# Weights' rounded high parts by a second transfer from GpSimd's queue, low parts on VectorE

## The chip, the cores and the metric

The kernel runs on 1 core of one Trainium2 chip. The metric is the device time of one execution in microseconds (us). Three runs of the kernel before took 629.13 us at the median, 628.03 to 631.23. One further execution was profiled; everything said of stretches and waits comes from it. What differs by less than 0.5% counts as no change.

## The reference

Two layers of a streaming encoder over 512 tokens of width 1024, in float32. Layer A is multi-head latent attention with a low-rank query and a low-rank key/value, a rotary key shared by 8 heads and a gate. Layer B is differential attention: two softmaxes per head, their weighted difference, a norm per head, a gate. Between them one shared K/V is projected from the residual stream.

```python
u = rmsnorm(h, pre_g); proj = u @ w_in                       # layer A
c_q, c_kv, k_r, z = split(proj, [768, 1280, 1344])
q = rmsnorm(c_q, q_norm_g) @ w_uq                            # 8 heads of 128 + 64 rotary
k_n = rmsnorm(c_kv) @ w_uk; v = rmsnorm(c_kv) @ w_uv
p = softmax(mask((q_n k_n + q_r k_r) * scale)); o = p @ v    # chunk-causal, chunk 64
h = h + rmsnorm((o * silu(z)) @ w_o, post_g)
k, v = split(rmsnorm(h) @ w_kv); k = rope(k)                 # shared K/V
q, z = split(rmsnorm(h) @ w_in); q = rope(q)                 # layer B
p = softmax(q1 k1) - lam * softmax(q2 k2); o = p @ v
o = rmsnorm(o, subln_g) * (1 - lam_init)
h = h + rmsnorm((o * silu(z)) @ w_o, post_g)
```

## The kernel before

Every product of weights is made of three passes on TensorE (PE): each operand is cut into a high part, rounded to PE's type `float32r`, and a low part, operand less high part, and `mm3` (L181 to L185) adds high x high, high x low and low x high into one PSUM tile. A weight block is 128 rows by up to 1024 columns (512 KB); a projection of one head with 1024 input channels takes 24 products of 128x128 by 128x512.

The class `Stream` holds all weight blocks in the order of their use. `load` (L80) brings a raw block by SyncE's (SP's) DMA queue into one of 2 buffers `wr`. `split` (L92) makes the high part in `wh` and the low part in `wl`, 3 buffers each, or in places of their own (`w1h`, `w1l` for the second half of the output projections, `sp` for some others). `ahead`, called behind each use, loads three and splits two blocks ahead of the block in use. So the high part of block k+3 can be written when PE's last product with the high part of block k is done.

Which engine splits is set by `eng`. For the first projection (g0, the compressed key/value) and the two blocks split with it, both parts come from VectorE (DVE). Behind L359 the high part is a `tensor_scalar` with 1.0 on GpSimd (POOL, L129) and the low part a subtraction on DVE (L132). In layer B the blocks of k and of the gate z have both parts on POOL, the blocks of q have the rule's.

POOL also multiplies the rotations' second halves by the sines (L374), scales exponentials by 1 / sum (L545 in layer A, L877 in layer B), sums squares (L343, L394, L407), applies the norm of some heads (L906) and stores the residual rows into `hdr` by its own DMA queue (L716). DVE does the rotations' other parts (L372, L373, L375), the scores' scaling with the maximum (L516), the weighted difference of the two softmaxes (L878) and all low parts of activations (L132, L832, L835). ScalarE (ACT) rounds activations and takes exponentials.

The tile framework's scheduler puts each engine's instructions in an order of its own, by a simulated timeline; on the chip each engine runs its instructions in that order, and an instruction that waits holds those behind it. Tiles in PSUM come from 8 buffers; a product into a new one waits until the old content was read.

Layer B's heads run as listed in `border`: the projections k0, q0, k1, z0, then the scores s0, then q1, k2, z1, z2, z3, and from then on for each head h the scores s(h+1), the projection q(h+2), the transposes t(h), k(h+3), perhaps a gate block, and the products with V, p(h).

Of the kernel before, what the change touches and what calls it, by code (L numbers as in the profile page):

```python
# [33 lines left out]
# columns of the small table  # L34
# [7 lines left out]
# 2*pi in parts of few bits, so that n * part is exact  # L42
# [16 lines left out]
def f(ap):  # L59
    return ap.bitcast(F32)  # L60


class Stream:
    """Weight blocks in the order of their use: loaded ahead, split one ahead."""

    def __init__(self, nc, raw, wh, wl):
        self.nc, self.rawp, self.pools = nc, raw, (wh, wl)
        self.units, self.raw, self.done = [], {}, {}
        self.n_load = self.n_split = self.n_get = 0
        self.eng = ("dve", "dve")  # L70
        self.first = {}     # the places of the first units
        self.tailed = set()

# [18 lines left out]
    def split(self, upto):  # L92
        self.load(upto)
        while self.n_split < min(upto, len(self.units)):
            k = self.n_split
            to = [self.units[k][1](n, k) for n in range(2)]
            if to[0] is None:       # its place isn't there yet
                return
            raw = self.raw.pop(k)
            kc, m = raw.shape[1], raw.shape[2]  # L100
            if k in self.tailed:    # the last 64 columns' low part goes behind their high part
                hi, lo = (t[:, None, :m + 64] for t in to)
                self.nc.vector.tensor_copy(hi[:, :, :m], raw)
                for a, o in ((0, lo[:, :, :m - 64]), (m - 64, hi[:, :, m:])):
                    v = slice(a, a + o.shape[2])
                    self.nc.vector.tensor_tensor(o, raw[:, :, v], f(hi[:, :, v]), op=ALU.subtract)
            else:
                hi, lo = (t[:, :kc * m].rearrange("p (k m) -> p k m", k=kc) for t in to)
                split(self.nc, hi, lo, raw, *(self.units[k][2] or self.eng))
            self.done[k] = (hi, lo)  # L110
            self.n_split += 1
# [12 lines left out]
def split(nc, hi, lo, src, eng="act", lo_eng="dve"):  # L124
    """hi = src to the product's type, lo = src - hi: exact together."""
# [16 lines left out]
def _body(ctx, tc, nc, ins, out, dbg):  # L142
# [38 lines left out]
    def mm3(o, w, x, first, last):  # L181
        """o += w^T x, each of w and x a (high, low) pair."""
# [4 lines left out]
    # ------------------------------------------------------------ first loads  # L187
# [4 lines left out]
    # the first chunk in two parts, for the products to start early  # L192
# [73 lines left out]
    # ------------------------------------------------------------ constants  # L266
# [12 lines left out]
    # products that nobody reads, to have TensorE's clock up when the first data come  # L279
# [9 lines left out]
    def rsqrt_rows(r, v2):  # L289
        """r = (2 v2)^-1/2 by the tables, then one step of Newton"""  # L290
# [15 lines left out]
    # ------------------------------------------------------------ x and the first projection  # L306
# [52 lines left out]
    ws.eng = ("pool", "dve")  # L359
# [8 lines left out]
    # ------------------------------------------------------------ c_q, and c_kv's norm beside it  # L368
    def rope(src, C, Sn, shuf):
        """the rotated src (PSUM) in a new tile"""  # L370
# [27 lines left out]
    # the rotary key: its weights' high part on one half of the rows, the low part on the other  # L398
# [40 lines left out]
    # ------------------------------------------------------------ the gate  # L439
# [25 lines left out]
    # ------------------------------------------------------------ V  # L465
    vh, vl = big_t("vh"), big_t("vl")      # [token, (tile, half), 512]
# [13 lines left out]
    # ------------------------------------------------------------ attention, layer A  # L480
# [24 lines left out]
    def softmax_part(h, tags, srcs, nscale):  # L505
        """masked scores (one PSUM tile per query tile) to exponentials and 1 / their sums"""
        e = [epool.tile([P, 1280], F32, tag="e", name=f"e{tag}{h}") for tag in tags]
        st = [[sm_t(n + tag) for n in ("mx", "l", "ri")] for tag in tags]
        for i in range(NT):
            n = P * (i + 1)  # L510
            one = slice(i, i + 1)
            for et, (mx, l, _), src in zip(e, st, srcs):
                ev = et[:, OFF[i]:OFF[i] + n]
                o = src(i)
                # the negated logits, their least, and exp(least - negated logit)
# [32 lines left out]
    PT = [(0, 0), (512, 1), (1024, 2), (896, 3)]     # where key tile j starts in the transposed tile  # L548
# [71 lines left out]
    def post(parts, done=None):  # L620
        """res += norm(o) * g, one token tile, by parts of its row: (o, g, res, a tile for o * g)"""
# [22 lines left out]
    def wo_end(norm, done, cut=False):  # L644
        """the last heads' products with w_o, one token tile after the other"""
# [9 lines left out]
        for i in range(NT):  # L655
            wo_half0(w, 7, [i])
            if cut and i == NT - 1:
                # in two parts, for the sums of squares to end early
# [16 lines left out]
    def attention(order, zg, proj, scores, norm, after):  # L675
        """the heads, one behind the other, and the first products with w_o beside the last ones"""
# [27 lines left out]
    # ------------------------------------------------------------ output projection A, h, its transpose  # L704
# [77 lines left out]
    # lambda  # L782
# [29 lines left out]
    # ------------------------------------------------------------ layer B: attention  # L812
# [42 lines left out]
    def scores_b(h):  # L855
# [3 lines left out]
        def src(i):  # L859
            """both scores' products: query high and low parts below each other, by the key's  # L860
            high part on either half of the rows, then the query's high part by the key's low part"""
# [22 lines left out]
    def subln_sq(h, o):  # L884
        sq = tmp_t("sqo")
        if h < H - 1:
            # the squares of either half of the rows, added, high and low part below each other
# [49 lines left out]
def _mt(w):  # L937
    """(K, 128 m) to [m, 128, K / 128, 128]"""
# [4 lines left out]
def _half(w):  # L943
    """(K, 1024) to [half, pair, 128, 2, 512]"""
# [66 lines left out]
```

## Time and profile before

| What | us |
|---|---|
| median of three runs (lowest, highest) | 629.13 (628.03, 631.23) |
| the profiled execution: span, the only time that its page gives | 628.3 |
| PE busy | 599.2 |
| DVE busy | 445.2 |
| ACT busy | 254.2 |
| POOL busy | 246.1 |
| share of the chain that ended last: PE, DVE, ACT, POOL, DMA | 69%, 15%, 5%, 3%, 2% |

The span runs from the first to the last instruction. Busy time counts the time in which an engine has an instruction running; DMA-issuing instructions are not counted. PEclk is the TensorE clock that was granted, as a share of full speed. The profile's idle times carry the name of what ended them. A row of a tile gives shortest, median and longest duration.

### The profile page before, as it was taken

What the parts mean: (1) busy time and instruction counts of PE and PEld (TensorE: products, weight loads), DVE (VectorE), ACT (ScalarE), POOL (GpSimd) and SP (SyncE); (2) the same over time, 40 slices, a digit from 0 to 9 for tenths busy, and PEclk for the clock granted to TensorE, in tenths of its full rate; (3) what the DMA queues carried; (4) which work ended last, traced back from release to release, by engine and by line L of the source; (5) the groups of instructions that cost most, each with busy time, mean ns of one, the idle gap of its engine ahead of it and who ended that gap; (6) DMA issues with size and microseconds to landing.
All of it is one profiled execution on the core that took longest, in us unless ns stands there. A gap on an engine that the chain in (4) does not pass through costs nothing.

```text
span 628.3 us, 7754 instructions
## 1 busy us (share of the span) xinstructions
PE 599.2 (95%) x2742; PEld 485.9 (77%) x2742; DVE 445.2 (71%) x790; ACT 254.2 (40%) x560; POOL 246.1 (39%) x232
## 2 busy tenths in 40 slices
PE   8998999999999999999999996999989999899995
PEld 6776888888888888788878884877768677587785
DVE  7997963346574758756775277748997897988754
ACT  6045411222343434313661124164645539637341
POOL 5251541113343231443232555737346554545100
PEclk9997999999999999999999997999889799699999
DMA  8132242312221223555312231140221121126102
GB/s 305 35 130 68 67 135 101 93 58 71 82 67 43 68 92 96 200 147 162 101 43 80 89 101 67 38 131 33 68 67 35 34 76 59 34 94 215 61 34 101
DMA packets 20119, 56.24 MB, mean 90 GB/s; under 512 B 2416, under 2 KB 3056, under 8 KB 20080
## 3 DMA queue, kind: packets, MB, share of 16 engines
q1 hardware_dynamic: 19296, 53.51, 26.9%
q0 software_dynamic: 640, 2.10, 0.9%
q8 instruction: 22, 0.36, 0.2%
q14 instruction: 17, 0.14, 0.1%
q10 hardware_dynamic: 144, 0.13, 0.1%
HBM read 51.53 MB, written 4.19 MB: 89 GB/s over the span
## 4 chain that ended last, share of the span: by engine, by line
PE 69%; DVE 15%; ACT 5%; issue 5%; POOL 3%; DMA 2%; SPq 1%; DVEq 0%; POOLq 0%; ACTq 0%
PE wo L183 4%; PE wo L185 4%; PE wo L184 4%; PE qb L183 3%; PE qb L184 3%; PE qb L185 2%; PE za L183 2%; PE za L184 2%; PE za L185 2%; DVE eb L878 2%; PE vb L183 2%; PE vb L184 2%; PE vb L185 2%; DVE ra L375 2%; PE cq L183 2%
## 5 line engine op out<-in xcount | busy, mean ns | idle before, releaser
L129 POOL TENSOR_SCALAR wh<-wr 128x1024 fp32r<-128x1024 f32 (+2 forms) x74 | 80.1, 1083 | 197.9 <-PE qb L184 31.3
L132 DVE TENSOR_TENSOR wl<-wr,wh 128x1024 fp32r<-128x1024 f32 (+2 forms) x60 | 72.6, 1211 | 34.6 <-POOL wh L129 34.5
L132 POOL TENSOR_TENSOR wl<-wr,wh 128x1024 fp32r<-128x1024 f32 x16 | 40.2, 2513 | 0.7
L375 DVE TENSOR_TENSOR ra<-ra,rb 128x512 f32<-128x512 f32 x21 | 32.1, 1527 | 5.4 <-POOL rb L374 5.4
L866 PE MATMUL sb<-k,q 128*128 128x128 f32 (+3 forms) x64 | 23.7, 419 | 11.7 <-DVE mxb L516 5.4
L545 POOL TENSOR_SCALAR ea<-ea,ria 128x128 f32<-128x128 f32 (+3 forms) x32 | 18.5, 595 | 36.5 <-DVE ria L522 36.5
L127 ACT ACTIVATE pth<-pt 128x512 fp32r<-128x512 f32 (+1 forms) x48 | 21.9, 529 | 25.0 <-PE pt L557 25.0
L878 DVE SCALAR_TENSOR_TENSOR eb<-eb,rib,ec 128x128 f32<-128x128 f32 (+3 forms) x32 | 30.7, 989 | 1.6 <-POOL ec L877 1.5
L877 POOL TENSOR_SCALAR ec<-ec,ric 128x128 f32<-128x128 f32 (+3 forms) x32 | 23.3, 744 | 18.4 <-DVE ric L874 15.5
L183 PE MATMUL qb<-hT2h,wh 128*128 128x512 f32 x64 | 30.1, 470 | 0.0
L184 PE MATMUL qb<-hT2l,wh 128*128 128x512 f32 x64 | 28.7, 448 | 0.0
L519 ACT ACTIVATE ea<-ea,mxa 128x128 f32<-128x128 f32 (+3 forms) x32 | 17.9, 560 | 25.9 <-DVE mxa L516 25.5
L185 PE MATMUL qb<-hT2h,wl 128*128 128x512 f32 x64 | 28.3, 441 | 0.0
L132 DVE TENSOR_TENSOR ptl<-pt,pth 128x512 fp32r<-128x512 f32 (+1 forms) x48 | 26.5, 590 | 1.8 <-ACT pth L127 1.8
L183 PE MATMUL wo<-w1h,ogh 128*128 128x512 f32 (+1 forms) x72 | 26.7, 371 | 0.0
L374 POOL TENSOR_TENSOR rb<-rb,SB 128x512 f32<-128x512 f32 x16 | 21.7, 1354 | 12.5 <-DVE rb L372 12.4
L185 PE MATMUL wo<-w1h,ogl 128*128 128x512 f32 (+1 forms) x72 | 26.5, 368 | 0.0
L183 PE MATMUL wo<-wh,ogh 128*128 128x512 f32 x64 | 25.4, 399 | 1.1 <-ACT ogh L127 1.1
L184 PE MATMUL wo<-w1l,ogh 128*128 128x512 f32 (+1 forms) x72 | 26.4, 366 | 0.0
L866 PEld LDWEIGHTS sb<-k,q 128*128 128x128 f32 x64 | 11.6, 202 | 18.8 <-DVE mxb L516 6.8
L183 PE MATMUL kb<-hT1h,wh 128*128 128x512 f32 x64 | 25.3, 396 | 0.0
L183 PE MATMUL za<-xh,wh 128*128 128x512 f32 x64 | 25.0, 391 | 0.0
(329 smaller groups left out, 1847.3 us busy)
## 6 DMA issues: line engine op xcount, KB each, us to landing
wr<-in_w_za SPq DMA_DIRECT2D x8, 512.0 KB, 3.6
wr<-in_w_oa SPq DMA_DIRECT2D x8, 512.0 KB, 3.6
wr<-in_w_vb SPq DMA_DIRECT2D x8, 512.0 KB, 3.6
wr<-in_w_kb SPq DMA_DIRECT2D x8, 512.0 KB, 3.5
wr<-in_w_qb SPq DMA_DIRECT2D x8, 512.0 KB, 3.5
wr<-in_w_zb SPq DMA_DIRECT2D x8, 512.0 KB, 3.5
wr<-in_w_ob SPq DMA_DIRECT2D x8, 512.0 KB, 3.7
wr<-in_w_cq SPq DMA_DIRECT2D x6, 512.0 KB, 3.5
```

What stands on the lines that cost most here:

```text
L127: nc.scalar.activation(hi, src, AF.Copy)
L129: nc.gpsimd.tensor_scalar(hi, src, 1.0, 1.0, op0=ALU.mult, op1=ALU.mult)
L132: (nc.vector if lo_eng == "dve" else nc.gpsimd).tensor_tensor(lo, src, f(hi), op=ALU.subtract)
L183: pe.matmul(o, w[0], x[0], start=first, stop=False)
L184: pe.matmul(o, w[0], x[1], start=False, stop=False)
L185: pe.matmul(o, w[1], x[0], start=False, stop=last)
L374: gps.tensor_tensor(b, b, Sn, op=ALU.mult)
L375: dve.tensor_tensor(a, a, b, op=ALU.add)
L545: gps.tensor_scalar(ev, ev, ri[:, i:i + 1], 1.0, op0=ALU.mult, op1=ALU.mult)
L866: pe.matmul(os[g][:, :n], qb[g][:, ti], kb[g][:, :n], start=True, stop=False)
L877: gps.tensor_scalar(e2[:, w], e2[:, w], r2[:, i:i + 1], 1.0, op0=ALU.mult, op1=ALU.mult)
L878: dve.scalar_tensor_tensor(e1[:, w], e1[:, w], r1[:, i:i + 1], e2[:, w], op0=ALU.mult, op1=ALU.subtract)
```

## The change

The stream gets a flag `cast`, set behind the first projection (where before the engines were set). With the flag, `split` begins a DMA on POOL's queue from the same place in DRAM into the high part's tile, whose type `float32r` has the transfer round, and the low part is a subtraction on DVE, whatever engines the block was added with. The raw block still comes by SP's queue; the low part needs both transfers. POOL makes no parts of weights any more. Comments of the file go too, and the lines behind L104 move down by up to 6 (L132 is L138, the rotation's L372 to L375 are L378 to L381, L516 is L522); the new transfer is L112 and the new subtraction L113.

```diff
@@ -61,15 +61,16 @@
         self.tailed = set()
+        self.cast = False
...
@@ -106,7 +107,12 @@
             else:
                 hi, lo = (t[:, :kc * m].rearrange("p (k m) -> p k m", k=kc) for t in to)
-                split(self.nc, hi, lo, raw, *(self.units[k][2] or self.eng))
+                if self.cast:
+
+                    self.nc.gpsimd.dma_start(hi, self.units[k][0])
+                    self.nc.vector.tensor_tensor(lo, raw, f(hi), op=ALU.subtract)
+                else:
+                    split(self.nc, hi, lo, raw, *(self.units[k][2] or self.eng))
             self.done[k] = (hi, lo)
...
@@ -356,7 +362,7 @@
-    ws.eng = ("pool", "dve")
+    ws.cast = True
```

The scheduler's order changes with it. PE's and SP's orders stay nearly as they were. Three places:

First extract: DVE behind the first projection, where the angles of layer B's rotation (`ang`, `SB`, `CB`) are made. `wl11` is the low part of the third block of c_q, `axl` and `akl` are low parts of sums of squares that PE adds up next. Before:

```order
L402 TENSOR_TENSOR kr_400<-g0_4_146,kr_400 128x512
L132 TENSOR_TENSOR wl11_453<-wr11_334,wh11_452 128x1024
L321 SCALAR_TENSOR_TENSOR ang_377<-n_379,ang_377 128x512
L322 TENSOR_SCALAR ang_377<-ang_377 128x512
L326 TENSOR_SCALAR SB_376<-SB_376,cols_90 128x512
L328 TENSOR_SCALAR CB_375<-CB_375,cols_90 128x512
L132 TENSOR_TENSOR wl12_489<-wr12_450,wh12_488 128x1024
L132 TENSOR_TENSOR axl_415<-acc_x_141,axh_414 128x512
```

and now:

```order
L408 TENSOR_TENSOR kr_400<-g0_4_146,kr_400 128x512
L327 SCALAR_TENSOR_TENSOR ang_377<-n_379,ang_377 128x512
L328 TENSOR_SCALAR ang_377<-ang_377 128x512
L113 TENSOR_TENSOR wl11_453<-wr11_334,wh11_452 128x1024
L332 TENSOR_SCALAR SB_376<-SB_376,cols_90 128x512
L334 TENSOR_SCALAR CB_375<-CB_375,cols_90 128x512
L138 TENSOR_TENSOR axl_415<-acc_x_141,axh_414 128x512
L138 TENSOR_TENSOR akl_419<-acc_kv_397,akh_418 128x512
```

The low part stands behind the last two steps of the angles, no longer ahead of them.

Second extract: POOL at the start of layer B, from the high part of k1's block (`wh65`) on; `wh66` is z0's, `wh67` q1's, `wh68` k2's, `wh69` z1's; each `rb` is the product with the sines in a rotation, `ec` the second softmax of head 0. Before:

```order
L129 TENSOR_SCALAR wh65_3121<-wr65_3064 128x1024
L132 TENSOR_TENSOR wl65_3122<-wr65_3064,wh65_3121 128x1024
L129 TENSOR_SCALAR wh66_3164<-wr66_3119 128x1024
L374 TENSOR_TENSOR rb_3105<-rb_3105,SB_376 128x512
L132 TENSOR_TENSOR wl66_3165<-wr66_3119,wh66_3164 128x1024
L129 TENSOR_SCALAR wh67_3210<-wr67_3162 128x1024
L374 TENSOR_TENSOR rb_3151<-rb_3151,SB_376 128x512
L129 TENSOR_SCALAR wh68_3242<-wr68_3208 128x1024
L374 TENSOR_TENSOR rb_3194<-rb_3194,SB_376 128x512
L132 TENSOR_TENSOR wl68_3243<-wr68_3208,wh68_3242 128x1024
L129 TENSOR_SCALAR wh69_3344<-wr69_3240 128x1024
L132 TENSOR_TENSOR wl69_3345<-wr69_3240,wh69_3344 128x1024
```

and now:

```order
L112 DMA wh65_3121<-in_w_kb 128x1024
L112 DMA wh66_3164<-in_w_zb 128x1024
L380 TENSOR_TENSOR rb_3105<-rb_3105,SB_376 128x512
L112 DMA wh67_3210<-in_w_qb 128x1024
L380 TENSOR_TENSOR rb_3151<-rb_3151,SB_376 128x512
L112 DMA wh68_3242<-in_w_kb 128x1024
L380 TENSOR_TENSOR rb_3194<-rb_3194,SB_376 128x512
L112 DMA wh69_3344<-in_w_zb 128x1024
L883 TENSOR_SCALAR ec0_3247<-ec0_3247,ric_3253 128x128
```

The order of high parts and rotations is the same; subtractions are gone from between them, and each high part is a transfer that POOL begins.

Third extract: DVE at the same place, from q0's rotation (`qb0`) over k1's (`kb1`) to the first scores of head 0 (`sb0_0_0`). Before:

```order
L373 TENSOR_TENSOR ra_3150<-qb0_3125,CB_375 128x512
L132 TENSOR_TENSOR wl67_3211<-wr67_3162,wh67_3210 128x1024
L375 TENSOR_TENSOR ra_3150<-ra_3150,rb_3151 128x512
L832 TENSOR_TENSOR q0_3156<-ra_3150,q0_3156 64x512
L832 TENSOR_TENSOR q1_3157<-ra_3150,q1_3157 64x512
L372 STREAM_SHUFFLE rb_3194<-kb1_3168 128x512
L373 TENSOR_TENSOR ra_3193<-kb1_3168,CB_375 128x512
L375 TENSOR_TENSOR ra_3193<-ra_3193,rb_3194 128x512
L835 TENSOR_TENSOR kl_3201<-ra_3193,k0_3199 64x512
L835 TENSOR_TENSOR kl_3201<-ra_3193,k1_3200 64x512
L516 ISA eb0_3246,mxb_3248<-sb0_0_0_3254,mask_126 128x128
L516 ISA mxb_3248 128x1
```

and now:

```order
L379 TENSOR_TENSOR ra_3150<-qb0_3125,CB_375 128x512
L381 TENSOR_TENSOR ra_3150<-ra_3150,rb_3151 128x512
L113 TENSOR_TENSOR wl67_3211<-wr67_3162,wh67_3210 128x1024
L838 TENSOR_TENSOR q0_3156<-ra_3150,q0_3156 64x512
L838 TENSOR_TENSOR q1_3157<-ra_3150,q1_3157 64x512
L378 STREAM_SHUFFLE rb_3194<-kb1_3168 128x512
L379 TENSOR_TENSOR ra_3193<-kb1_3168,CB_375 128x512
L381 TENSOR_TENSOR ra_3193<-ra_3193,rb_3194 128x512
L113 TENSOR_TENSOR wl68_3243<-wr68_3208,wh68_3242 128x1024
L841 TENSOR_TENSOR kl_3201<-ra_3193,k0_3199 64x512
L841 TENSOR_TENSOR kl_3201<-ra_3193,k1_3200 64x512
L522 ISA eb0_3246,mxb_3248<-sb0_0_0_3254,mask_126 128x128
```

q1's low part (`wl67`) has moved behind q0's rotation, and k2's (`wl68`), which POOL made, stands behind k1's. A third one, z0's (`wl66`), stands a few rows ahead behind k0's rotation, where there was none.

## Rows read from the trace of the kernel before

**Rows 1.** The page, part 1: busy us, share of the span, instructions of each engine.

```profile
PE 599.2 (95%) x2742; PEld 485.9 (77%) x2742; DVE 445.2 (71%) x790; ACT 254.2 (40%) x560; POOL 246.1 (39%) x232
```

**Rows 2.** PE's waits over the span: us in total, times, longest us.

```profile
PE sb L866 <- DVE mxb L516: 5.4, 2, 4.8
PE ssx L415 <- ACT axh L127: 4.0, 1, 4.0
```

**Rows 3.** Busy time by stretch, PE alone: stretch, length, busy (instructions), granted clock, DMA share, GB/s.

```profile
45.00:60.00 15.00, 11.03 (x35) 0.77 0.27 89
380.00:395.00 15.00, 10.18 (x33) 0.77 0.21 70
435.00:450.00 15.00, 14.26 (x51) 0.77 0.12 36
460.00:480.00 20.00, 17.93 (x76) 0.83 0.18 54
485.00:500.00 15.00, 13.55 (x45) 0.77 0.12 36
...
535.00:550.00 15.00, 13.11 (x35) 0.66 0.11 36
```

**Rows 4.** DVE's instructions in order of time: start, us, line, operation, tiles.

```profile
41.07 1.71 DVE L132 TENSOR_TENSOR wl<-wr,wh 128x1024 fp32r<-128x1024 f32 x1
...
364.39 2.87 DVE L375 TENSOR_TENSOR ra<-ra,rb 128x512 f32<-128x512 f32 x1 [0.91 <-POOL rb L374]
...
371.37 1.82 DVE L132 TENSOR_TENSOR wl<-wr,wh 128x1024 fp32r<-128x1024 f32 x1
373.12 1.53 DVE L375 TENSOR_TENSOR ra<-ra,rb 128x512 f32<-128x512 f32 x1
...
378.81 2.84 DVE L375 TENSOR_TENSOR ra<-ra,rb 128x512 f32<-128x512 f32 x1 [0.68 <-POOL rb L374]
...
383.65 2.19 DVE L835 TENSOR_TENSOR kl<-ra,k 64x512 fp32r<-64x512 f32 x1 [0.56 <-ACT k L830]
```

**Rows 5.** POOL's instructions in order of time: z0's cast, two of the 16 subtractions.

```profile
361.99 1.06 POOL L129 TENSOR_SCALAR wh<-wr 128x1024 fp32r<-128x1024 f32 x1 [1.69 <-PE kb L184]
...
378.74 2.37 POOL L132 TENSOR_TENSOR wl<-wr,wh 128x1024 fp32r<-128x1024 f32 x1
...
457.18 2.70 POOL L132 TENSOR_TENSOR wl<-wr,wh 128x1024 fp32r<-128x1024 f32 x1
```

**Rows 6.** DVE by shape, 350 to 600 us (busy us, mean ns), then two tiles' rows (shortest/median/longest ns).

```profile
L375 DVE TENSOR_TENSOR ra<-ra,rb 128x512 f32<-128x512 f32 x16 | 27.4, 1714 | 3.0 <-POOL rb L374 2.9
...
L835 DVE TENSOR_TENSOR kl<-ra,k 64x512 fp32r<-64x512 f32 x16 | 14.6, 916 | 5.2 <-ACT k L830 5.1
...
L375 DVE TENSOR_TENSOR ra<-ra,rb x21: 674/1446/2884, 72.6 to 556.7; 128x512 f32<-128x512 f32 x21
...
L132 DVE TENSOR_TENSOR wl<-wr,wh x60: 681/1220/2312, 32.3 to 585.8; 128x1024 fp32r<-128x1024 f32 x40, 128x768 fp32r<-128x768 f32 x12, 128x512 fp32r<-128x512 f32 x8
```

**Rows 7.** POOL by shape, 350 to 600 us: count, busy us, mean ns, idle before.

```profile
L132 POOL TENSOR_TENSOR wl<-wr,wh 128x1024 fp32r<-128x1024 f32 x15 | 37.8, 2521 | 0.6
L129 POOL TENSOR_SCALAR wh<-wr 128x1024 fp32r<-128x1024 f32 x27 | 32.1, 1188 | 49.8 <-PE qb L184 31.3 <-PE kb L184 6.9 <-PE vb L185 6.3
```

**Rows 8.** DMA issues: POOL's issuing instruction (ns), then count, KB each, us to landing.

```profile
L716 POOL DMA_DIRECT2D hdr<-xr x8: 539/568/741, 292.9 to 317.5; - x8
...
hdr<-xr POOLq DMA_DIRECT2D x8, 256.0 KB, 2.6
...
wr<-in_w_za SPq DMA_DIRECT2D x8, 512.0 KB, 3.6
```

**Rows 9.** Busy time by stretch: PE, PEld, DVE, ACT, POOL, then clock, DMA share, GB/s.

```profile
0.00:15.70 15.70, 13.27 (x53) 10.35 (x53) 11.31 (x16) 10.52 (x17) 8.77 (x16) 1.00 0.89 305
...
100.00:150.00 50.00, 50.00 (x223) 41.40 (x222) 21.10 (x26) 9.73 (x12) 9.49 (x10) 1.00 0.25 77
...
250.00:295.00 45.00, 44.02 (x220) 36.94 (x219) 30.60 (x51) 13.62 (x38) 17.42 (x20) 1.00 0.57 180
```

## The prediction

> **What bounds the kernel now.** I read the page's busy times first: TensorE (PE) is busy for 599.2 of 628.3 us, VectorE (DVE) for 445.2, GpSimd (POOL) for 246.1 [rows 1]. The whole span is PE's, so only two things can be won: time in which PE stands still, and time in which its clock is low. The clock line of the page shows where: it dips near the start and then in the last third. Next I read the list of PE's own waits: the two longest are 5.4 us on DVE's scores reduction, 4.8 of them at once, and 4.0 us on ScalarE (ACT) for the first sum of squares [rows 2]. Then the stretches around these and the shorter ones, with PE's busy time and granted clock [rows 3]. In each of the 15 us stretches 45-60, 380-395, 435-450 and 485-500 the mean clock is 0.77, so 0.23 x 15 = 3.45 us of full speed are lost there, on top of idle times of 4.0, 4.8, 0.7 and 1.5 us. 460-480 has 2.1 idle and 0.17 x 20 = 3.4 lost, 535-550 has 1.9 idle and 0.34 x 15 = 5.1 lost. The granted clock goes to its lower level (1.2 for 2.4 GHz) behind an idle moment of PE, even one of 0.7 us. So idle and clock together are worth 15.0 + 22.3 = 37 us: that is about all that a change beside PE can win here.
>
> Who makes PE wait? The scores' last product waits for a PSUM buffer that DVE has to read first. Its instructions are long in layer B: the rotation's add of two SBUF tiles takes 1714 ns on average, while the same add took 674 ns at its shortest; one of those long ones starts at 378.81 and lasts 2.84 us, and a POOL low-part subtraction starts at 378.74 and lasts 2.37 us [rows 4, 5, 6]. DVE's two-input instructions stand still while POOL reads SBUF.
>
> **The change part by part.** (1) POOL loses its 84 casts and 16 subtractions (2.52 us each): in 350-600 us alone 32.1 + 37.8 = 70 us, a cast taking 1.19 us there [rows 7]. (2) POOL gains 84 transfers. The only transfers POOL issues before are the eight of hdr, 0.57 us each at the median (0.54 to 0.74), and they land in 2.6 us for 256 KB; SP's of 512 KB land in 3.6 us [rows 8]. For a rounding transfer of 512 KB the trace has no row. Bounds: 2.6 us from the smaller plain one, and double the 3.6, 7.2 us, if rounding halves the pace; I take 4, nearest to the plain one. (3) DVE gains 16 subtractions at 1.22 us = 19.5 us (the median of those before; the longest took 2.3 [rows 6]).
>
> What (1) gives DVE from 350 to 600 us: the 16 adds (1714 - 690) x 16 = 16.4 us, the halves of k 16 x (0.92 - 0.69) = 3.7 us, those of q (same shape and number) counted as much, and of the weighted differences, which mostly chase POOL's scaling of the same head and keep that, I count 3 us [rows 6]. That is 27 us against 19.5 us added: DVE is relieved by 7 us net. This is small; it is the places that matter.
>
> Place 1, 45.9 to 50.0 us: PE waits for ACT, which waits for DVE's angles. At 41.07 a low part of 1.71 us stands in front of the last angle steps [rows 4]. The order now has it behind them (first extract of the change). Gain 1.7 us. 2.3 us of waiting stay, and with them the low clock, since 0.7 us were enough for that at 435-450.
>
> Place 2, 381.4 to 386.2 us, the first scores of layer B. DVE's queue before their first reduction has rotation adds of 2.87, 1.53 and 2.84 us, one low part of 1.82 us and a half of k of 2.19 us [rows 4], with POOL's work beside them [rows 5]; at 0.69 (adds, halves) and 1.22 us these are 7.3 us shorter. The order puts two more low parts there, and all three now stand right behind a rotation (third extract). That is early: the transfer for z0 can begin when k0's products are through, at 361.99 as the cast did [rows 5], and the rotation takes 0.7 + 0.7 us on DVE, some 0.9 us of waiting for POOL and 0.7 us again, 3 us. With 0.6 us of issue and L = 4 the rounded half is there 4.6 us behind the release, so DVE stands for 1.6 us at each of the three, and then subtracts for 1.22 us. I replayed the queue with these lengths: k0's add ends at 364.9, z0's low part at 367.8, k0's halves at 369.2, q0's add at 371.9, q1's low part at 373.2, q0's halves at 374.6, k1's add at 377.3, k2's low part at 378.6, k1's halves at 380.0. Before, the last of them ended at 385.84 [rows 4]; PE ran out of buffers at 381.4. So the wait of 4.8 us goes, and the low clock behind it: 4.8 + 3.45 = 8.2 us, for L up to 4.5; each further us of L gives back up to 3.
>
> Places 3 to 6 (435, 460, 485, 535 us): 0.7 + 2.1 + 1.5 + 1.9 = 6.2 us of waiting and 15.4 us of clock, 21.6 us [rows 3]. Before the second of them the rotation stood behind a POOL subtraction of 2.70 us [rows 5]. Each needs 0.7 to 2.1 us less, and each of the 8 heads has more contention than that (27 / 8 = 3.4 us); against it stand two added low parts per head (2.4 us), and that DVE now stands at three low parts per head where the rounded half is not there yet. I count that half of it goes: 10.8 us.
>
> New costs: the rounded halves (64 blocks of 512 KB, 12 of 384, 8 of 256) add 40.4 MB to what the queues carry. From 250 to 295 us the queues moved 180 GB/s x 45 us = 8.1 MB, and 12 rounded blocks bring 6.3 MB: 14.4 MB. The fastest stretch of the trace is the first, 305 GB/s [rows 9]; at that rate 14.4 MB take 47 us, 2 us more than there are. For waits of DVE on landings outside the six places I add 4 us.
>
> The Trainium skill bears on two of these terms. SBUF — State Buffer, Who interferes with whom, says that a VectorE instruction with two SBUF inputs is held by a GpSimd instruction that reads SBUF, wholly and until it ends, and not by one that only writes; the 2.84 beside 2.37 us above agree for the first half, and no run here shows the second. By it a DMA instruction holds nobody and the 27 us all go; if a DMA instruction of 0.57 us held DVE as the cast of 1.19 us did, about half of what the casts caused would stay and DVE would gain nothing. DMA: Bandwidth & Descriptors, Specifications, gives about 358 GB/s from HBM per core; by it 14.4 MB fit into 40 us and my 2 us fall away, but the trace shows no stretch above 305.
>
> Sum: -1.7 - 8.2 - 10.8 + 2 + 4 = -14.7 us. The profiled execution's span is 628.3 us, the only time that the page gives of it, 0.8 under the median of the runs (629.13), so 628.3 - 14.7 + 0.8 = 614 us.
>
> **The rivals.** *The subtractions eat the relief.* DVE is the engine that PE waits for, and it gets 16 more instructions in just the stretch where it is fullest. If POOL's DMA instructions hold DVE too, or the low parts stand in front of scores reductions, places 3 to 6 stay, and place 2 keeps its clock loss: -1.7 - 4.8 + 6 = 0, 629 us (623 to 633). For it speaks the small net of 7 us; against it, that before each late score the long instruction was one held by POOL.
>
> *The rounded half lands late (slower).* A high part was ready about 1.2 us after its buffer came free; now it is there after 0.6 + L. In layer B the low parts stand 3 us behind that moment, with the scores' reductions queued behind them on DVE, and PE waits for those. For L = 4 that is 1.6 us each, which the relief covers; from L = 5.5 on it no longer does: at L = 7 DVE stands for 4.6 us at each of three low parts per head, 14 us, of which some 2 us fall into waits for ACT and 3.4 us are the relief; of the 8.6 us left I count half, since DVE is not busy all the time: 4 us more for each of 7 heads, 629 - 2 + 28 = 655 us; at L = 6 half of that, 641. (The stages before layer B hold longer: with three buffers a unit of 5.4 us keeps pace while 0.6 + L + 1.22 + 5.4 is under 3 x 5.4, L under 9.) Against it: 2.6 us for POOL's transfers of 256 KB. For it: no row has a rounding transfer, and two transfers now share the queues.
>
> *Nothing late at all.* If all six places vanish and only the 6 us of new costs come, 629.1 - 37 + 6 = 598 us.
>
> *The change is not done as said* would be transfers that don't run ahead because POOL's queue is blocked. A transfer waits for the same release (PE's last product with that buffer) as the cast did, and the rotations behind it need a later product, so this I give no chance of its own.
>
> **How the numbers follow.** Forecast 614 us (its own range 603 to 623) 0.53; all gone, under 603, 0.08; the subtractions eat it, 623 to 633, 0.19; late landing, above 633, 0.20. A measurement of this kernel tells some 0.5% (3.1 us) from no change: under 626 is faster, over 632.3 slower. Faster 0.53 + 0.08 + 0.05 of the third = 0.66, same 0.13, slower 0.21. The range 600 to 641 leaves out the best 5% and the worse half of the late landings.
>
> **What would show it.** Right: rotation adds near 0.7 us, no PE wait and a full clock at the first scores of layer B, POOL busy about half of before, landings of 4 us. Wrong: DVE idle for several us on a transfer before a low part, landings beyond 5.5 us, PE waits for low parts in the gate stage, or adds that stay over 1 us beside POOL's DMA instructions.

## The result, and the profile after

The changed kernel takes 612.44 us in the median of four runs (609.05 to 614.15), the kernel before 628.58 us beside it (626.74 to 631.23). The ratio is 0.973, 95% interval 0.971 to 0.976. The forecast was 614 us.

The page's busy times and its line of the granted clock, of the profiled execution (span 607.0 us), answer to [rows 1]:

```profile
PE 589.6 (97%) x2742; PEld 481.4 (79%) x2742; DVE 420.1 (69%) x806; ACT 255.0 (42%) x560; POOL 158.8 (26%) x216
...
PEclk9998999999999999999999999999999699799999
```

PE does the same 2742 instructions. Its idle time falls from 628.3 - 599.2 = 29.1 us to 607.0 - 589.6 = 17.4 us. The mean granted clock rises from 0.963 to 0.982; times the span, the loss of full speed falls from 23.2 to 10.9 us. That is 24 us together for 21.3 us of span (idle moments under a low clock count twice). So all of the gain lies where the prediction looked for it, in PE's idle time and its clock.

PE's waits (us in total, times, longest), where [rows 2] had 5.4 and 4.0 us:

```profile
PE sb L872 <- DVE q L838: 4.7, 4, 2.5
...
PE ssx L421 <- ACT axh L133: 0.7, 1, 0.7
```

PE's busy time and clock in the stretches of [rows 3] (length, busy, clock, DMA share, GB/s), and 515-530, which is new:

```profile
45.00:60.00 15.00, 13.73 (x50) 0.89 0.62 200
380.00:395.00 15.00, 15.00 (x68) 1.00 0.48 142
435.00:450.00 15.00, 15.00 (x71) 1.00 0.53 163
460.00:480.00 20.00, 16.50 (x54) 0.74 0.26 79
485.00:500.00 15.00, 15.00 (x70) 1.00 0.54 174
515.00:530.00 15.00, 13.73 (x46) 0.77 0.33 107
535.00:550.00 15.00, 15.00 (x68) 1.00 0.82 261
```

These are stretches of time, and in layer B the changed kernel comes to the same products 5 to 20 us earlier: 460-480 and 515-530 hold the scores of heads 4 and 6, which stood at 485 and 535 before. So the comparison has to go by product. PE's idle time + its lost clock, (1 - clock) x length, from the start of one head's scores to that of the next (start and sums in us):

| scores of head | 0 | 1 | 2 | 3 | 4 | 5 | 6 | 7 |
|---|---|---|---|---|---|---|---|---|
| before, start | 378 | 417 | 434 | 462 | 485 | 514 | 534 | 565 |
| before | 4.8 + 3.4 | 0 | 0.7 + 3.4 | 2.1 + 3.4 | 1.5 + 3.4 | 1.0 + 0 | 1.9 + 5.1 | 0 |
| changed, start | 373 | 404 | 422 | 447 | 465 | 497 | 517 | 545 |
| changed | 0 | 0 | 0.3 + 0 | 0 | 3.5 + 5.1 | 0.5 + 0 | 0.9 + 3.4 | 0 |

Heads 0 and 3 wait no longer, head 2 hardly, head 6 less than before, and head 4 longer. DVE's instructions by shape from 350 to 600 us (count, busy us, mean ns, idle before them) answer to [rows 6]:

```profile
L113 DVE TENSOR_TENSOR wl<-wr,wh 128x1024 fp32r<-128x1024 f32 x27 | 33.1, 1227 | 13.8 <-DMA wh<-in_w_kb 6.1 <-issue 2.9 <-DMA wh<-in_w_zb 2.4
L838 DVE TENSOR_TENSOR q<-ra,q 64x512 fp32r<-64x512 f32 x16 | 13.3, 832 | 0.5
L841 DVE TENSOR_TENSOR kl<-ra,k 64x512 fp32r<-64x512 f32 x16 | 12.8, 798 | 3.0 <-ACT k L836 2.7
L381 DVE TENSOR_TENSOR ra<-ra,rb 128x512 f32<-128x512 f32 x16 | 11.0, 688 | 3.2 <-POOL rb L380 3.2
```

The 16 adds fell from 1714 to 688 ns, the length forecast for an add beside which GpSimd reads nothing. The transfers (count, KB each, us from issue to landing), of which [rows 8] had no row:

```profile
wh<-in_w_za POOLq DMA_DIRECT2D x8, 512.0 KB, 4.5
...
wh<-in_w_kb POOLq DMA_DIRECT2D x8, 512.0 KB, 3.8
wh<-in_w_qb POOLq DMA_DIRECT2D x8, 512.0 KB, 4.4
```

### The profile page after: what moved, and what is told of

Read it like the earlier page. It is cut to its first block, busy times and chain, and to the rows that moved or that the text cites. A ratio compares the mean times of both kernels' runs of the same rounds, so it can differ in the third digit from the quotient of the medians.

```text
span 607.0 us, 7782 instructions
## 1 busy us (share of the span) xinstructions
PE 589.6 (97%) x2742; PEld 481.4 (79%) x2742; DVE 420.1 (69%) x806; ACT 255.0 (42%) x560; POOL 158.8 (26%) x216
## 3 DMA queue, kind: packets, MB, share of 16 engines
q0 software_dynamic: 12736, 42.47, 22.7%
## 4 chain that ended last, share of the span: by engine, by line
PE 79%; DVE 10%; ACT 3%; DMA 3%; issue 3%; POOL 1%; SPq 1%; DVEq 0%; POOLq 0%
PE wo L189 5%; PE wo L190 5%; PE wo L191 5%; PE sb L872 3%; PE qb L189 3%; PE za L189 2%; PE vb L189 2%; PE za L191 2%; PE vb L191 2%; PE vb L190 2%; PE za L190 2%; PE sb L875 2%; PE qb L190 2%; PE qb L191 2%; PE pt L563 2%
## 5 line engine op out<-in xcount | busy, mean ns | idle before, releaser
L113 DVE TENSOR_TENSOR wl<-wr,wh 128x1024 fp32r<-128x1024 f32 (+2 forms) x74 | 84.2, 1137 | 81.5 <-issue 20.1
L138 DVE TENSOR_TENSOR ptl<-pt,pth 128x512 fp32r<-128x512 f32 (+1 forms) x48 | 26.7, 591 | 2.1 <-ACT pth L133 1.9
L189 PE MATMUL qb<-hT2h,wh 128*128 128x512 f32 x64 | 27.7, 433 | 0.0
L872 PE MATMUL sb<-k,q 128*128 128x128 f32 (+3 forms) x64 | 22.7, 404 | 4.7 <-DVE q L838 4.7
L190 PE MATMUL qb<-hT2l,wh 128*128 128x512 f32 x64 | 26.5, 415 | 0.0
L191 PE MATMUL qb<-hT2h,wl 128*128 128x512 f32 x64 | 26.4, 412 | 0.0
L190 PE MATMUL wo<-wl,ogh 128*128 128x512 f32 x64 | 25.2, 393 | 0.0
L189 PE MATMUL zb<-hT2h,wh 128*128 128x512 f32 x64 | 25.0, 390 | 0.0
L191 PE MATMUL kb<-hT1h,wl 128*128 128x512 f32 x64 | 25.0, 390 | 0.0
L190 PE MATMUL kb<-hT1l,wh 128*128 128x512 f32 x64 | 24.9, 390 | 0.0
L191 PE MATMUL zb<-hT2h,wl 128*128 128x512 f32 x64 | 24.9, 390 | 0.0
L191 PE MATMUL za<-xh,wl 128*128 128x512 f32 x64 | 24.9, 389 | 0.0
```

The costliest lines, as they stand in the source:

```text
L113: self.nc.vector.tensor_tensor(lo, raw, f(hi), op=ALU.subtract)
L138: (nc.vector if lo_eng == "dve" else nc.gpsimd).tensor_tensor(lo, src, f(hi), op=ALU.subtract)
L189: pe.matmul(o, w[0], x[0], start=first, stop=False)
L190: pe.matmul(o, w[0], x[1], start=False, stop=False)
L191: pe.matmul(o, w[1], x[0], start=False, stop=last)
L872: pe.matmul(os[g][:, :n], qb[g][:, ti], kb[g][:, :n], start=True, stop=False)
```

## The experiments

Theory: a GpSimd instruction that reads SBUF holds VectorE's instructions with two SBUF inputs, and the gain is that 84 casts and 16 subtractions no longer do so. Rivals: only the long subtractions count (A); the transfer itself is the gain (B); later ones are in the expectations.

**One part at a time.** First the low parts alone:

```
-  ws.add(ins[f"w_{nm}b"][h], None, None if nm == "q" else ("pool", "pool"))     (kernel before)
+  ws.add(ins[f"w_{nm}b"][h], None, None)
```

> The kernel before with one part of the change alone: the 16 low parts of w_kb and w_zb go from GpSimd to VectorE, the 84 casts stay on GpSimd, no rounded transfer. Theory (every GpSimd instruction that reads SBUF holds VectorE's two-input instructions): of the 70 us of GpSimd work that leaves 350-600 us in the full change, this removes 38 (the subtractions) and keeps 32 (the casts), so about half of the gain of 16.7 us, some 620 us (616 to 624); the rotation's adds come out between 0.69 and 1.71 us, near 1.0. Rival A (only the 2.5 us subtractions matter, the 1.2 us casts are too short to): the whole gain, 612 us, adds at 0.7 us. Rival B (the gain is the transfer's, the high part being ready without an engine): no gain, 627 to 632, since VectorE only gets 16 x 1.2 us more.

Measured: 624.28 us (ratio 0.994, 0.992 to 0.997). Then the transfer alone:

```
-  self.nc.vector.tensor_tensor(lo, raw, f(hi), op=ALU.subtract)                 (changed kernel)
+  eng = self.nc.gpsimd if self.units[k][2] else self.nc.vector
+  eng.tensor_tensor(lo, raw, f(hi), op=ALU.subtract)
```

> The changed kernel with the other part alone: the high parts come by the rounding transfer, but the 16 low parts of w_kb and w_zb stay on GpSimd. Theory (reads by GpSimd hold VectorE): the 32 us of casts go from 350-600 us, the 38 us of subtractions stay, so the other half of the gain, some 621 us (617 to 625), with rotation adds still over 1.2 us where a subtraction stands beside them. Rival A (only the subtractions matter): no gain, 627 to 632. Rival B (the gain is the transfer's): 612 us with adds that stay long.

Measured: 620.08 us (0.985, 0.980 to 0.991). Then no transfer, but GpSimd relieved all the same:

```
-  ws.eng = ("pool", "dve")                                                       (kernel before,
+  ws.eng = ("act", "dve")                                                         low parts as in the first)
```

> The kernel before with the 84 casts on ScalarE in place of GpSimd and all low parts on VectorE, no rounded transfer: GpSimd reads as little SBUF as in the changed kernel, and the queues carry as little as before. Theory (reads by GpSimd hold VectorE): adds at 0.7 us as in the changed kernel; ScalarE gets 84 casts of some 1.1 us (0.53 for 512 columns), 92 us on 255, which puts some of its other work late: 610 to 620 us. Rival B (the gain is the transfer's, and only that): 627 us or more. If ScalarE's casts stand before the exponentials at the scores, 620 to 630 with the waits named ScalarE.

Measured: 616.88 us (0.982, 0.975 to 0.988). DVE by shape from 350 to 600 us, of the low parts alone, the transfer alone and the casts on ACT in turn:

```profile
L132 DVE TENSOR_TENSOR wl<-wr,wh 128x1024 fp32r<-128x1024 f32 x27 | 39.8, 1473 | 8.9 <-POOL wh L129 8.8
...
L375 DVE TENSOR_TENSOR ra<-ra,rb 128x512 f32<-128x512 f32 x16 | 12.9, 805 | 0.0
```

```profile
L382 DVE TENSOR_TENSOR ra<-ra,rb 128x512 f32<-128x512 f32 x16 | 13.8, 865 | 4.5 <-POOL rb L381 4.4
```

```profile
L375 DVE TENSOR_TENSOR ra<-ra,rb 128x512 f32<-128x512 f32 x16 | 10.9, 680 | 0.0
```

Without any rounding transfer the adds come to 680 ns and the kernel wins 11 of the 16 us: rival B is out as the whole story, and so is A, since the transfer alone, with all 16 subtractions still on GpSimd, wins 8. What the other 5 us are, ACT's added casts or the transfer itself, these runs do not separate. That the product with the sines comes sooner on a shorter GpSimd queue is not it: DVE stands 3.0 us before the adds in the kernel before [rows 6] and 3.2 in the changed one. The parts make 3.9 and 8.1 us where the whole makes 16.1. The low parts alone came out just outside the slow edge of what the theory said (616 to 624), with adds at 805 ns and not near 1.0 us. Where each part acts is seen when PE's idle time and its lost clock, (1 - clock) x length, are summed by slices of 5 us (idle + clock, us):

| | 40-70 us | 360-400 us | 400-560 us |
|---|---|---|---|
| before | 4.0 + 3.4 | 4.8 + 3.4 | 7.2 + 15.5 |
| changed | 1.3 + 1.7 | 0 + 0 | 5.2 + 8.5 |
| low parts alone | 4.0 + 3.4 | 0.6 + 0 | 8.1 + 18.9 |
| transfer alone | 1.5 + 0 | 0 + 0 | 9.1 + 13.6 |
| casts on ACT | 2.2 + 1.7 | 0.1 + 0 | 4.9 + 17.4 |

Either part alone cures the first scores of layer B; the first wait needs the casts gone; the idle time of the late scores falls only when both are gone. The stretch 400-560 of the transfer alone and of the changed kernel:

```profile
400.00:560.00 160.00, 150.85 (x643) 0.91 0.39 133
```

```profile
400.00:560.00 160.00, 154.74 (x682) 0.95 0.45 145
```

**Reads and writes put back.** GpSimd gets instructions of no use behind each transfer, which read the raw block, or only write:

```
+  self.nc.gpsimd.tensor_scalar(out, p, 1.0, 1.0, op0=ALU.mult, op1=ALU.mult)     (p: half of raw; out: scratch)
+  self.nc.gpsimd.memset(out, 0.0)                                                (in its place, second run)
```

> The changed kernel with GpSimd's reading put back without its use: behind each of the 84 transfers GpSimd multiplies the raw block by one into a scratch tile that nobody reads (two instructions of half a block, about 0.6 us each, as long together as the cast of 1.19 us). Theory (GpSimd instructions that read SBUF hold VectorE's two-input instructions): VectorE's low parts go from 1.23 back to about 1.46 us, the first wait for ScalarE near 46 us comes back in part, and the time goes towards that of the run with the casts kept and only the low parts moved, 624.3: 619 to 626 us. Rival D (what counted was that the high part is there without waiting for GpSimd's queue, not the holding): 611 to 614 us, with the low parts at 1.23.

Measured: 640.62 us (1.018, 1.013 to 1.024), beyond what any theory said. These instructions stood on GpSimd's queue for 190 us in all, waiting for raw blocks, and PE's longest single wait was for a GpSimd result (4.2 us, for hTf). So the run measures a blocked queue as much as reading, and tells the theories apart badly; the low parts (1257 ns) came nowhere near 1460.

> The same place and number of extra GpSimd instructions as in the run with the reads put back, but they only write (a memset of the same scratch tile). Theory (only reading holds): VectorE's instructions as long as in the changed kernel, 610 to 615 us, although GpSimd gets 84 x 2 more instructions. Rival E (any GpSimd instruction beside VectorE holds it, or what comes behind on GpSimd's queue, the rotation's product and the scaling, comes late): as slow as with the reads, 619 to 626 us, where the memsets last as long; in proportion if they are shorter.

Measured: 619.61 us (0.983, 0.977 to 0.988); its edges reach what the theory said, its median does not. DVE's rows of layer B were as in the changed kernel (687, 832 and 798 ns). But the memsets, which wait for nothing, all ran between 2.0 and 151.7 us, at the start of GpSimd's queue, and not where I had put them in the code. The next pair was to be in layer B alone, with a read that waits for nothing either:

```
+  for _ in range(self.extra):          # 2 from layer B's first block on
+      self.nc.gpsimd.tensor_scalar(self.scr, self.const, 1.0, 1.0, op0=ALU.mult, op1=ALU.mult)
+      self.nc.gpsimd.memset(self.scr, 0.0)                                       (in its place, second run)
```

> The changed kernel with GpSimd reads put back in layer B alone, and without a new wait: from layer B's first block on, behind each rounding transfer GpSimd multiplies a constant tile (the mask, 512 columns) by one into a scratch tile that nobody reads, twice. The instructions wait for no transfer, unlike those of the run that read the raw blocks, which stood 150 us for landings. Theory (reads hold): the adds, q's and k's halves and the low parts get longer in 340-580 us (means up by 0.05 to 0.2 us), and the waits of PE before the late scores grow: 3 to 10 us over the changed kernel of the same chip, 613 to 622 us. Rival D (the holds don't matter, place and order do): the changed kernel's time within 2 us.

> The same places and number of added instructions in layer B, but memsets of the scratch tile (0.54 us each in the run before), which read nothing. Theory (only reads hold): VectorE's rows as in the changed kernel to 0.02 us, and the time within 3 us of it on the same chip, 608 to 615 us. In the run with memsets everywhere the rows were unchanged too, but the time 619.6, with 3.7 us idle at the first sums of squares: if that came from the start of the program, it is gone here; if GpSimd's mere activity costs, it is as slow as the reads.

> The changed kernel once more, word for word, for the comparison on the same chip: 608 to 613 us by its earlier runs (612.4 median of 4), and by the run with the late low parts (608.8), whose instructions stand in the same order on every engine.

Measured on one chip: reads 625.31 us (0.995, 0.992 to 0.997), writes 617.13 us (0.981, 0.979 to 0.984), the changed kernel again 610.85 us (0.972, 0.968 to 0.976). Both lie further above the changed kernel than was said (some 14 us, not 3 to 10; 6.3 us, not within 3), and not by the place meant: the 60 instructions ran from 2.3 to 96.9 us in the first and from 2.0 to 72.7 us in the second, and layer B's rows stayed as they were. So the test is in the first stage, where DVE has the same instructions in all three. First the run with reads: one row of GpSimd (16 reads in a row, 23.95 to 38.57 us), then rows of DVE beside it:

```profile
23.95 14.62 POOL L115 TENSOR_SCALAR scr<-mask 128x512 f32<-128x512 f32 x16
...
28.04 0.87 DVE L105 CAST wh<-wraw 128x576 fp32r<-128x576 f32 x1
28.83 1.08 DVE L108 TENSOR_TENSOR wl<-wraw,wh 128x512 fp32r<-128x512 f32 x1
29.84 0.63 DVE L108 TENSOR_TENSOR wh<-wraw,wh 128x64 fp32r<-128x64 f32 x1
...
33.82 0.71 DVE L327 TENSOR_SCALAR n<-ang 128x512 f32<-128x512 f32 x1
```

The run with writes, 20 memsets in a row (19.62 to 32.84 us):

```profile
19.62 13.22 POOL L115 MEMSET scr<- 128x512 f32 x20
...
24.92 0.79 DVE L105 CAST wh<-wraw 128x576 fp32r<-128x576 f32 x1
25.63 0.67 DVE L108 TENSOR_TENSOR wl<-wraw,wh 128x512 fp32r<-128x512 f32 x1
26.23 0.21 DVE L108 TENSOR_TENSOR wh<-wraw,wh 128x64 fp32r<-128x64 f32 x1
...
28.98 0.71 DVE L327 TENSOR_SCALAR n<-ang 128x512 f32<-128x512 f32 x1
```

The repetition of the changed kernel, GpSimd standing idle from 19.75 to 35.44 us:

```profile
23.16 0.45 DVE L104 CAST wh<-wraw 128x576 fp32r<-128x576 f32 x1
23.53 0.68 DVE L107 TENSOR_TENSOR wl<-wraw,wh 128x512 fp32r<-128x512 f32 x1
24.13 0.22 DVE L107 TENSOR_TENSOR wh<-wraw,wh 128x64 fp32r<-128x64 f32 x1
...
26.64 0.43 DVE L324 TENSOR_SCALAR n<-ang 128x512 f32<-128x512 f32 x1
```

This is the theory seen directly: the subtraction of two SBUF tiles takes 0.68 us beside nothing, 0.67 beside a writer and 1.08 beside a reader (0.22, 0.21 and 0.63 for 64 columns). The Trainium skill, SBUF — State Buffer, Who interferes with whom, says just that of two-input instructions, and its second half (a writer does not hold them), of which the prediction had no row, agrees here. The same section says that casts and tensor_scalar instructions can, in some of their modes, hold and be held by GpSimd too; the rows agree: 0.45 against 0.79 and 0.43 against 0.71 us beside a writer. That is one way in which memsets cost 6 us at the start; I had left DVE's one-input instructions out of the theory.

**What is left in layer B.** PE waits in the changed kernel before the scores of heads 2, 4 and 6. DVE in order of time before the longest of these waits (PE stands from 464.9 to 467.35 us):

```profile
459.90 1.23 DVE L884 SCALAR_TENSOR_TENSOR eb<-eb,rib,ec 128x256 f32<-128x256 f32 x1
...
461.65 1.27 DVE L884 SCALAR_TENSOR_TENSOR eb<-eb,rib,ec 128x384 f32<-128x384 f32 x2
462.84 1.21 DVE L113 TENSOR_TENSOR wl<-wr,wh 128x1024 fp32r<-128x1024 f32 x1
463.98 0.68 DVE L381 TENSOR_TENSOR ra<-ra,rb 128x512 f32<-128x512 f32 x1
...
465.90 2.98 DVE L838 TENSOR_TENSOR q<-ra,q 64x512 fp32r<-64x512 f32 x2
```

and GpSimd's rows beside the last of these, both of instructions that read SBUF:

```profile
465.40 1.26 POOL L380 TENSOR_TENSOR rb<-rb,SB 128x512 f32<-128x512 f32 x1 [1.94 <-DVE rb L378]
466.70 1.63 POOL L912 TENSOR_TENSOR zb<-zb,rs 128x512 f32<-128x512 f32 x1
```

PE waits for q's low halves, and they are held once more, by the reads that GpSimd still does. From 456.27 us, when DVE takes up q's product, to the last of these halves it is not idle, and in the 10 us before the waits of heads 2 and 6 it stands for no landing either: late transfers do not stand directly behind these three waits. Two runs take the reads away:

```
-  gps.tensor_tensor(b, b, Sn, op=ALU.mult)                                       (rotation; both runs)
+  dve.tensor_tensor(b, b, Sn, op=ALU.mult)
-  gps.tensor_scalar(e2[:, w], e2[:, w], r2[:, i:i + 1], 1.0, ...)                (second run only, as is
+  act.activation(e2[:, w], e2[:, w], AF.Copy, scale=r2[:, i:i + 1])               dve for gps in zg * rs)
```

> The changed kernel with the rotation's product by the sine table (1.28 us on GpSimd, reading two SBUF tiles, 24 of them) moved to VectorE (0.68 us each by the same shape there). In the changed kernel the two subtractions of q's low half at 465.9 us take 2.98 us for both beside such a product and a scaling on GpSimd, and PE runs out of score buffers there. Theory (reads by GpSimd hold VectorE): these come down to 1.4 us, the handover to GpSimd and back goes, VectorE gets 16 us more but loses as much in holds: the PE wait at 465 shrinks from 3.5 us to under 2, 606 to 612 us. Rival C (VectorE's own work is what counts, it is the fullest in layer B): 16 x 0.68 = 11 us more in layer B, of which half is seen by PE, 615 to 620 us.

> The changed kernel with nearly all of GpSimd's reading in layer B gone: the rotation's product by the sine table on VectorE (0.68 us, 24 of them), the scaling of the second exponentials on ScalarE (a copy with a scale, 32 of 0.2 to 0.7 us) and the scalings of the gated rows (5) on VectorE. Theory (reads hold): VectorE's weighted differences, 0.84 us for 512 columns in the changed kernel, come to about 0.7, q's halves to 0.69, and the waits of PE at the late scores, 5.2 us with 8.5 us of low clock behind, go by half or more: 601 to 607 us. Rival C (VectorE and ScalarE are full enough there that their own added work is seen): 610 to 620 us.

Measured: 608.45 us (0.969, 0.965 to 0.973) and 609.72 us (0.970, 0.965 to 0.976). The rows went to their floor, as in the second run:

```profile
L838 DVE TENSOR_TENSOR q<-ra,q 64x512 fp32r<-64x512 f32 x16 | 11.0, 686 | 0.5
L381 DVE TENSOR_TENSOR ra<-ra,rb 128x512 f32<-128x512 f32 x16 | 10.9, 683 | 0.2
```

but PE's waits for q did not go: 4.9 us in that run's list (profiled in the slowest of its four executions), where the changed kernel has 4.7. They moved. Before head 4's scores PE waits 1.8 us in the first run, under the 2 us said, and 1.7 in the second, where the changed kernel has 3.5; before heads 2 and 6, where the changed kernel has 0.3 and 0.9, it waits 0.8 and 0.3 us in the first run and not at all in the second. But before head 7, where the changed kernel has no wait, 2.1 and 3.2 us are new. In the second run DVE stood there for the landing of a rounded block, with q's halves behind it:

```profile
541.99 1.22 DVE L113 TENSOR_TENSOR wl<-wr,wh 128x1024 fp32r<-128x1024 f32 x1 [3.64 <-DMA wh<-in_w_ob]
...
545.09 1.41 DVE L838 TENSOR_TENSOR q<-ra,q 64x512 fp32r<-64x512 f32 x2
```

So the holds by GpSimd can account for about half of the longest wait, not for all of it (the order of PE's and DVE's instructions changed too). The first run's time is in the range said, the second's is not (601 to 607): new waits stand in the place of the old. Two more runs asked what else makes them:

```
-  self.nc.vector.tensor_tensor(lo, raw, f(hi), op=ALU.subtract)                  (first run: issued one unit
+  self.pend[k] = (lo, raw, hi)                                                    later, from ahead() or get())
-  border += [("z", z) for z in {1: [4], 3: [5], 5: [6, 7]}.get(h, [])]           (second run)
+  border += [("z", z) for z in {1: [4], 2: [5], 4: [6], 5: [7]}.get(h, [])]
```

> The changed kernel with each low part one unit later in VectorE's program than its rounding transfer was begun (the transfers at the same place): VectorE no longer comes to a low part before its high part has landed. In the changed kernel VectorE stands 19 us before low parts from 340 to 580 us, 14 of them for landings. Theory (these waits lie where PE is not waiting: in 455 to 470 us, before the largest wait left, VectorE was never idle): within 3 us of the changed kernel, 609 to 615 us, with the waits for landings gone. Rival F (the landings are what is late at the last scores): under 606 us. If a low part is now late for its product, PE waits for wl and the time is over 616.

> The changed kernel with the gate's products of layer B spread: those of blocks 4 to 7 behind heads 1, 2, 4 and 5 in place of 1, 3, 5 and 5. In the changed kernel PE's waits left in layer B lie at 422, 465 and 515 us, before the scores of heads 2, 4 and 6, just where no gate product (5.6 us of PE work) stands between the last key product and the scores; PE waits there for the query's low half on VectorE (2.5 us). Theory (VectorE's queue between the query's product and its low half is longer than what PE has in between): the waits at 465 and 515 go, a smaller one comes before head 5 (490 us), which has lost its gate product: 3 to 9 us under the changed kernel, 602 to 608 us. Rival: the wait only moves to head 5 at full size and the clock falls as often: within 2 us.

Measured: 608.81 us (0.969, 0.965 to 0.972) and 610.98 us (0.971, 0.968 to 0.975). The first edit turned out to change nothing: every engine's instructions stand in the same order as in the changed kernel, since the scheduler places them by its own reckoning. It is a repetition of the changed kernel, and tells nothing of landings. In the second the time is the changed kernel's, as its rival said, and PE still waits for q: 5.7 us in the profiled execution, the slowest of its six. By head, the waits moved with the gate's products: heads 4 and 6, which got one ahead of their scores, wait no more; head 5, which lost one, now waits 2.1 us, and head 7, which lost one of two, 3.1 us. So PE waits where it has too little to do between q's product and the scores, while DVE works off its queue up to q's low half. The holds lengthen that queue by a part; what would end the waits as a whole no run shows.

No version is shown to beat the changed kernel. Over its own four runs, the four of the edit that changed nothing and the six of the repetition its median is 610.3 us (607.05 to 614.73), and 608.45 lies within that.

## Why the prediction was right

**What bounds the kernel, and the hold.** Right. Adds went to 688 ns (690 was used), and a subtraction of the same size is lengthened by GpSimd's reads and not by its writes. The relief of 27 us was not made up as counted: beside the adds' 16.4 us, the halves of k and q fell by 1.8 and 1.1 us, not by 3.7 each, and the weighted differences of 256 to 512 columns by 8.1 us (27.6 to 19.5), not by 3.

**Place 1.** Right in kind, mis-sized: -1.7 forecast; 7.4 us of idle time and clock became 3.0, and 1.4 + 0 in the repetition. Only the low part in front of the angles was counted. But GpSimd's casts, and the sums of squares that stood behind them, held the angle steps too: three of them took 3.84 us before and 3.13 after, the last 1.78 and 1.17 us. The clock, too, was not sure to fall with the wait that stays: it cost 1.7 us in the first profile and nothing in the repetition. The kernel before showed as much, since head 5's wait of 0.7 us left its clock full (514 to 531 us).

**Place 2.** Right: -8.2 forecast, -8.2 measured. The replay's last half ended at 380.0; after, with the program 5.3 us ahead by then, it ends 373.74 + 1.40 = 375.14 us:

```profile
361.53 1.23 DVE L113 TENSOR_TENSOR wl<-wr,wh 128x1024 fp32r<-128x1024 f32 x1 [1.77 <-DMA wh<-in_w_zb]
...
366.92 1.22 DVE L113 TENSOR_TENSOR wl<-wr,wh 128x1024 fp32r<-128x1024 f32 x1
...
372.60 1.23 DVE L113 TENSOR_TENSOR wl<-wr,wh 128x1024 fp32r<-128x1024 f32 x1 [0.21 <-DMA wh<-in_w_kb]
373.74 1.40 DVE L841 TENSOR_TENSOR kl<-ra,k 64x512 fp32r<-64x512 f32 x2
```

The stand of 1.6 us before each of three low parts was seen once (1.77); the others were 0 and 0.21.

**Places 3 to 6.** Nearly right in size (-10.8 forecast; 22.7 became 13.7, -9.0, over 400-560), but not as put: not half of each place. Head 3's place (460) went whole, 5.5 us, and head 2's (435) nearly, from 4.1 to 0.3; head 6's (535) fell from 7.0 to 4.3, and head 4's (485) grew from 4.9 to 8.6 us. That these add up to nearly the half that was counted is luck.

**The transfer.** Right: L = 4 was taken, 3.8 to 4.5 us measured at the median of the weights shown (over 5 us, up to 10.9, only for blocks of w_oa, w_vb and w_ob that come in bursts), and an issue takes 0.56 to 0.59 us at the median of layer B's three weights. The late landing as a rival had its condition (5.5 us) met by no block of k, q or z there (4.8 us at most); only in the run with most of GpSimd's reads gone did a landing stand ahead of a wait of PE, that of a block of w_ob before head 7.

**New costs.** Wrong: +6 forecast, none found. In the fullest stretch PE stands at no time:

```profile
250.00:295.00 45.00, 45.00 (x226) 1.00 0.84 295
```

and the small waits of 70-360 and 560-600 us (3.1 us before) came to 0.1, and to 1.7 in the repetition. The 305 GB/s that I took as the ceiling was misread, too: it is the mean of a stretch that begins with the program (32 GB/s in the first 2 us), and from 6 to 16 us the queues of the kernel before moved 388 GB/s.

So the sum met the measured time in part by luck, with two errors that cancel: some 10 us too little from New costs and places that were not counted, against a profile whose execution was the fastest of its four. On the profiled executions the change is -21.3 us, not -14.7; between medians it is -16.1. Nor was the 0.8 us right that led from span to median: the runs last 1.7 to 2.4 us longer than their spans, so the profiled execution of before lay some 1 us above its median.

## What to carry to other kernels

Before moving work to GpSimd, list which DVE instructions on the critical path will run beside it: a GpSimd instruction that reads SBUF can hold a DVE subtraction or add of two SBUF tiles beside it, and it is the sum over all such readers that counts, since removing one kind alone left the idle time of the late scores no smaller. Compare waits by product and not by time since the start, since an earlier gain shifts all that follows. A cast of a weight block costs no engine at all if the transfer does it, for 0.6 us of issue and a second reading of the block from HBM. And look where an added instruction really ran before its time is read: three of these experiments acted at another place than the code had them at, and one not at all.

## What was not expected of the hardware

The queues moved more than the 305 GB/s that the prediction took for the fastest. One stretch of the kernel before (all engines' busy times, then clock, DMA share and GB/s):

```profile
6.00:16.00 10.00, 8.32 (x34) 5.95 (x33) 9.68 (x10) 8.11 (x14) 7.45 (x5) 1.00 1.05 388
```

Two of the changed kernel:

```profile
250.00:265.00 15.00, 15.00 (x81) 13.00 (x81) 8.11 (x18) 4.62 (x12) 5.97 (x11) 1.00 1.05 377
...
545.00:555.00 10.00, 10.00 (x41) 7.06 (x42) 7.65 (x23) 9.86 (x24) 1.80 (x2) 1.00 1.08 400
```

The Trainium skill, DMA: Bandwidth & Descriptors, Specifications, gives about 358 GB/s from HBM for a core, half of what it gives for the stack that two cores share; here one core runs. In the last stretch the issues are loads of w_ob and of the hidden rows, and 400 is above the page's figure; the measurement decides. Landings were longer there (7.6 to 10.0 us at the median).

PE's clock fell four times without an idle moment ahead of it: twice with the casts on ACT (at 453 and 556 us), once with the gate's products spread (479 us), and once in the run with memsets behind every transfer, here before and after 511 us:

```profile
505.00:511.00 6.00, 6.00 (x30) 0.99 0.57 175
511.00:517.00 6.00, 6.00 (x13) 0.50 0.26 87
```

And the same idle time cost different amounts of clock: 4.9 us in 400-560 went with 17.4 us lost with the casts on ACT (its two falls without an idle moment among them), 5.2 us with 8.5 us in the changed kernel. Why is open. It is much of why executions of one program differ: the repetition's were 607.09 us at a mean clock of 0.984 and 614.73 us at 0.966.
